# Five rearrangements around the mixer of a streaming trunk: the sample's recurrence in two units, half B's columns loaded in 320s, its decay later, cache copies and recurrences queued elsewhere

## The chip, the core and the metric

The kernel runs on one core of a Trainium2 chip. The metric is the device time of one execution in microseconds (us). The engines are TensorE (PE, with PEld its loads of weights), VectorE (DVE), ScalarE (ACT), GpSimd (POOL) and SyncE (SP), which here only issues transfers. Each engine works through its own instructions in a fixed order; a wait on one holds what stands behind it there.

## The reference

One step of a two-layer encoder on 1024 new prompt frames and 64 frames of a running stream (the sample). All is float32, model width 1024.

- Layer 0: one input projection feeds mixer A (RWKV-7: 8 heads of 64, a matrix state per head and a recurrence over the frames) and mixer B (GLA: gated linear attention over chunks of 64 frames). Their outputs, side by side, go through one output projection `w_out_mix`; then x <- LN(alpha x + f(x)), a SwiGLU with its own norm.
- Layer 1: banded softmax attention. The prompt's chunks see themselves and 8 chunks back; the sample sees a cache of 128 rows of K and V (`cache_c_k`, `cache_c_v`). Then projection, norm, SwiGLU, norm.

```python
p = x @ w_in_mix                                  # both mixers
ya, wkv, shift = rwkv7_time_mix(p[..., :A_PROJ], ...)
yb, gla        = gla_mix(p[..., A_PROJ:], ...)
x = layer_norm(ALPHA * x + concat([ya, yb]) @ w_out_mix)
x = layer_norm(ALPHA * x + swiglu(x, w_in, w_out))
```

## The kernel before

The frames are worked in two halves. Half A holds 384 prompt frames and the 64 sample frames (448 columns), half B the other 640 prompt frames (two banks of 320 columns). x is held transposed, in 8 tiles `kt` of 128 features, and every product with weights is exact to float32 by three matmuls on a high and a low part: xh wh, xl wh, xh wl (L124 to L126 with the weights stationary, L135, L136 and L138 with x stationary). ACT casts the high part (L101 for weights, L215 for x, L113 in a general `split`), DVE or POOL subtracts for the low part (L106 or L108, L216, L114).

`load_w` brings a weight tile (512 KB) into one of two raw buffers `wr`, and keeps four split ones. `load_xt(1)` uses the same two raw buffers for half B's x^T, 8 tiles of 640 columns (`xraw`, L214). Three of the 8 split tiles of half B have buffers of their own (`xeh`, `xel`); the other five take over the buffers of half A's x^T, so that their casts can be made only when half A's projection has read those.

The run of layer 0:

1. `inproj_rwkv(0)` and `inproj_gla(0)`: half A's projections. Beside them run the recurrences of half A as generators: `rwkv` takes units of work through the stages rw1 (decay, gates, L437 to L467), rw1b (products within a chunk, L484 to L497), rw2 (a triangular inverse by steps of pairs L549 and L551 on 16 partitions, fed by a round through DRAM: `l_d`, `lt`), rw3 (state and output, L607 to L642) and rw4 (transposition, L649, store to `yg_d`). A unit is a pair of heads `p` and two chunks of 64 frames. The sample has one chunk only: four units of one chunk each, whose inverse works on 8 partitions.
2. `inproj_gla(1)`, beginning with its decay branch (L352: a product with a low-rank matrix, its copy, then L363), then the q, k, v gemms; `inproj_rwkv(1)`.
3. `load_xt(0, yg_d)`: half A's mixer output comes back as x^T, `pack` copies the 64 sample columns, high and low, side by side into `xpk` (ACT L852, POOL L853), and `proj` multiplies with `w_om`, into the accumulators `acc` (L825 to L829). Four steps (`PRE`) of half B's recurrences are written ahead of it, the rest behind it.
4. `layer_norm` of half A, token tile by token tile (L884 to L897), with transposition (L902) and split (L113, L114) into x^T for the FFN of half A, during which half B's recurrences go on.
5. `cache_setup`, written in the FFN at j = 8: four loads of cached V into `cv` (one buffer, L1125), each split into `cvh` by ACT L113 and DVE L114 and stored (L1128); then K.

A scheduler takes the program as written and sets the order of each engine by its own model of times; a step may so land far from where it is written. `tc.issue_after(ins)` puts what a block traces behind the instruction `ins` on the engine of `ins`, without a wait. Before the change it isn't used at these places.

## Time and profile before

| | |
|---|---|
| runs | 3104.43, 3107.47, 3107.52 us; median 3107.47 |
| profiled execution | 3102.95 us; its span 3101.2 us |
| PE / PEld busy | 3007.5 / 2676.5 us |
| DVE / ACT / POOL busy | 2016.0 / 1270.8 / 1366.7 us |
| mean granted clock of TensorE | 0.977 of full speed |
| moved | 399 MB, 129 GB/s |

TensorE is busy nearly all the time; what a stage can still give is its waits and the stretches in which it runs at the lower clock. So the profile is read by stretches: where TensorE stood, what ended it, and at what clock it went on.

### The profile page before, as it was taken

What the parts mean: (1) busy time and instruction counts of PE and PEld (TensorE: products, weight loads), DVE (VectorE), ACT (ScalarE), POOL (GpSimd) and SP (SyncE); (2) the same over time, 40 slices, a digit from 0 to 9 for tenths busy, and PEclk for the clock granted to TensorE, in tenths of its full rate; (3) what the DMA queues carried; (4) which work ended last, traced back from release to release, by engine and by line L of the source; (5) the groups of instructions that cost most, each with busy time, mean ns of one, the idle gap of its engine ahead of it and who ended that gap; (6) DMA issues with size and microseconds to landing.
All of it is one profiled execution on the core that took longest, in us unless ns stands there. A gap on an engine that the chain in (4) does not pass through costs nothing.

```text
span 3101.2 us, 50069 instructions
## 1 busy us (share of the span) xinstructions
PE 3007.5 (97%) x17468; PEld 2676.5 (86%) x17468; DVE 2016.0 (65%) x4941; ACT 1270.8 (41%) x2761; POOL 1366.7 (44%) x1489
## 2 busy tenths in 40 slices
PE   8999999899999999999999999999999999899998
PEld 7888888688888888798999898898899988899987
DVE  5677875879898764455554466245566668866667
ACT  4454554344454334243443132355444434333322
POOL 2354534444454334343342233244445546654444
PEclk9999999889999999999999999999899999999999
DMA  6553334533533228343342222866454443322212
GB/s 195 148 161 115 109 110 124 146 104 106 151 105 106 91 97 294 118 153 120 113 134 98 82 95 101 247 200 175 121 153 135 117 175 122 122 86 80 98 68 75
DMA packets 298492, 399.29 MB, mean 129 GB/s; under 512 B 125504, under 2 KB 218552, under 8 KB 298240
## 3 DMA queue, kind: packets, MB, share of 16 engines
q1 hardware_dynamic: 297088, 393.48, 41.2%
q8 instruction: 138, 2.26, 0.3%
q10 hardware_dynamic: 1152, 2.62, 0.2%
q14 instruction: 114, 0.93, 0.1%
HBM read 323.63 MB, written 75.51 MB: 129 GB/s over the span
## 4 chain that ended last, share of the span: by engine, by line
PE 77%; DVE 8%; DMA 7%; POOL 2%; issue 2%; ACT 2%; SPq 1%; POOLq 0%; ACTq 0%; DVEq 0%
PE gps L124 11%; PE gps L126 11%; PE gps L125 11%; PE gps L135 7%; PE gps L136 7%; PE gps L138 7%; PE gps L1065 3%; PE gps L1066 3%; PE gps L1067 3%; PE op L1328 2%; PE tp L1302 2%; DVE t L549 1%; DVE x L551 1%; PE sps L1286 1%; PE sps L1287 1%
## 5 line engine op out<-in xcount | busy, mean ns | idle before, releaser
L108 POOL TENSOR_TENSOR wl<-wr,wh 128x512 fp32r<-128x512 f32 (+2 forms) x297 | 521.7, 1760 | 669.3 <-ACT wh L101 612.0
L124 PE MATMUL gps<-xh,wh 128*128 128x320 f32 (+1 forms) x2188 | 747.7, 342 | 12.5 <-ACT xh L215 6.0
L125 PE MATMUL gps<-xl,wh 128*128 128x320 f32 (+1 forms) x2188 | 746.5, 341 | 0.6 <-DVE xl L216 0.6
L126 PE MATMUL gps<-xh,wl 128*128 128x320 f32 (+1 forms) x2188 | 745.9, 341 | 0.3 <-DVE wl L106 0.2
L101 ACT CAST wh<-wr 128x1024 fp32r<-128x1024 f32 x360 | 375.6, 1048 | 465.9 <-PE gps L125 135.6
L106 DVE TENSOR_TENSOR wl<-wr,wh 128x512 fp32r<-128x512 f32 (+2 forms) x297 | 293.8, 990 | 242.2 <-ACT wh L101 239.8
L124 PEld LDWEIGHTS gps<-xh,wh 128*128 128x128 f32 x2188 | 415.6, 190 | 34.4 <-ACT xh L215 6.0
L126 PEld LDWEIGHTS gps<-xh,wl 128*128 128x128 f32 x2188 | 415.6, 190 | 18.6 <-issue 0.8
L125 PEld LDWEIGHTS gps<-xl,wh 128*128 128x128 f32 x2188 | 415.5, 190 | 18.3 <-DVE xl L216 1.0
L1297 POOL TENSOR_SCALAR s<-s,mx 128x640 f32<-128x640 f32 (+5 forms) x144 | 205.3, 1426 | 258.7 <-DVE mx L1296 236.3
L138 PE MATMUL gps<-wh,xl 128*128 128x512 f32 x661 | 258.9, 397 | 5.4 <-DVE xl L216 4.8
L135 PE MATMUL gps<-wh,xh 128*128 128x512 f32 x661 | 259.9, 399 | 3.9 <-DVE acc L829 1.9
L136 PE MATMUL gps<-wl,xh 128*128 128x512 f32 x661 | 261.5, 397 | 0.0
L135 PE MATMUL gps<-wh,hh 128*128 128x512 f32 x572 | 224.8, 396 | 1.6 <-ACT wh L101 1.3
L136 PE MATMUL gps<-wl,hh 128*128 128x512 f32 x572 | 225.5, 396 | 0.0
L827 DVE TENSOR_TENSOR acc<-acc,gps 128x512 f32<-128x512 f32 x216 | 143.6, 680 | 89.6 <-PE gps L138 82.3
L138 PE MATMUL gps<-wh,hl 128*128 128x512 f32 x484 | 189.6, 397 | 1.6 <-DVE hl L943 1.6
L549 DVE TENSOR_TENSOR t<-lt,x 16x48 f32<-16x48 f32 (+9 forms) x540 | 149.3, 276 | 36.0 <-DMA lt<-l_d 25.5
L1295 ACT ACTIVATE s<-s,mx 128x640 f32<-128x640 f32 (+5 forms) x144 | 96.4, 669 | 149.6 <-DVE mx L1294 145.2
L138 PEld LDWEIGHTS gps<-wh,xl 128*128 128x128 f32 x661 | 124.9, 189 | 33.8 <-DVE xl L216 5.4
L135 PEld LDWEIGHTS gps<-wh,xh 128*128 128x128 f32 x661 | 125.0, 190 | 32.8 <-issue 2.5
L136 PEld LDWEIGHTS gps<-wl,xh 128*128 128x128 f32 x661 | 125.2, 189 | 28.0 <-DVE wl L106 1.1
(406 smaller groups left out, 6312.0 us busy)
## 6 DMA issues: line engine op xcount, KB each, us to landing
wr<-in_w_fi SPq DMA_DIRECT2D x176, 512.0 KB
wr<-in_w_fo SPq DMA_DIRECT2D x88, 512.0 KB
wr<-in_w_in SPq DMA_DIRECT2D x44, 512.0 KB
wr<-in_w_qk SPq DMA_DIRECT2D x32, 512.0 KB
wr<-in_w_o SPq DMA_DIRECT2D x24, 512.0 KB
qs<-qd SPq DMA_DIRECT2D x32, 320.0 KB
wr<-in_w_om SPq DMA_DIRECT2D x16, 512.0 KB
wr<-in_w_v SPq DMA_DIRECT2D x16, 512.0 KB
```

Of the source, the lines that this page charges most:

```text
L101: self.A.copy(hi, raw)
L106: self.V.tensor_tensor(lo[:, :h], raw[:, :h], hi[:, :h].bitcast(F32), op=ALU.subtract)
L108: self.G.tensor_tensor(lo[:, h:], raw[:, h:], hi[:, h:].bitcast(F32), op=ALU.subtract)
L124: self.T.matmul(ps, hi[:, kt, :], xh, start=(kt == 0), stop=False)
L125: self.T.matmul(ps, hi[:, kt, :], xl, start=False, stop=False)
L126: self.T.matmul(ps, lo[:, kt, :], xh, start=False, stop=(kt == nk - 1))
L135: self.T.matmul(ps, xh, wh, start=(i == 0), stop=False)
L136: self.T.matmul(ps, xh, wl, start=False, stop=(lo is None and i == n - 1))
L138: self.T.matmul(ps, cols(lo(kt)), wh, start=False, stop=(i == n - 1))
L549: V.tensor_tensor(tv, lt[:, j, w:16].unsqueeze(2).to_broadcast([m, r, w]), x[:, 0, j, 0:w].unsqueeze(1).to_broadcast([m, r, w]), op=ALU.mult)
L827: self.V.tensor_tensor(a, a, ps[:m], op=ALU.add)
L1297: G.tensor_scalar(s[:m, :nk], s[:m, :nk], mx[:m, 3:4], None, op0=ALU.mult)
```

## The change

It has these parts:

- **Sample units.** The sample's four units become two, each of two pairs of heads; `rw1`, `rw3`, `rw4` and `rwkv` take a list of pairs (`u.segs`). The inverse of such a unit works on 16 partitions.
- **Half B's x^T** comes as 16 loads of 320 columns into 8 buffers of the pool `yr` instead of 8 loads of 640 into the two raw buffers of the weights.
- **Decay of half B** stands behind its four q and k gemms instead of ahead of them; half A's stays.
- **`pack`** copies in two halves of four `kt`, the later half first.
- **Recurrences of half B** behind the four first steps are queued on DVE behind `norms[-2]`, the last scaling (L897) of the third of four token tiles of the norm.
- **`cache_setup`** is queued on SP behind the last weight load that is written before it, and on ACT behind its cast.

```diff
@@ __init__
+        self.norms = []
@@ load_w
-        self.A.copy(hi, raw)
+        self.last_cast = self.A.copy(hi, raw).ins
@@ inproj_gla
+        def decay():
...
+        if hf == 0:
+            decay()
...
+        if hf:
+            decay()
@@ rw1
-    def rw1(self, sp, p, n, g0):
+    def rw1(self, sp, ps, n, g0):
...
-        u = SimpleNamespace(p=p, n=n)
-        pc = slice(128 * p, 128 * p + 128)
+        w = 64 * n
+        W = w * len(ps)
+        n *= len(ps)
+        u = SimpleNamespace(n=n, segs=[(p, slice(w * i, w * i + w)) for i, p in enumerate(ps)])
...
@@ rw3
-        G.tensor_copy(u.sv[0:64, 0], S)
+        step = n // len(u.segs)
+        for i, (p, _) in enumerate(u.segs):
+            G.tensor_copy(u.sv[0:64, i * step], S[p])
+        out = {}
...
@@ rwkv
-        units = [(p, n, 64 * c, 0) for c in range(0, (PA, NB)[hf] // 64, n) for p in range(4)]
+        units = [((p,), n, 64 * c, 0) for c in range(0, (PA, NB)[hf] // 64, n) for p in range(4)]
         if hf == 0:
-            units = [(p, 1, SMP, 1) for p in range(4)] + units
+            units = [((p, p + 1), 1, SMP, 1) for p in (0, 2)] + units
...
@@ pack
-        self.A.copy(xs[:, :, 0:64], xt.hi[:, :, SMP:])
-        self.G.tensor_copy(xs[:, :, 64:128], xt.lo[:, :, SMP:])
+        for ks in (slice(4, 8), slice(0, 4)):
+            self.A.copy(xs[:, ks, 0:64], xt.hi[:, ks, SMP:])
+            self.G.tensor_copy(xs[:, ks, 64:128], xt.lo[:, ks, SMP:])
@@ layer_norm
-                    V.scalar_tensor_tensor(a[:, c], a[:, c], rstd, gb[:m, 1, c], op0=ALU.mult, op1=ALU.add)
+                    self.norms.append(V.scalar_tensor_tensor(a[:, c], a[:, c], rstd, gb[:m, 1, c], op0=ALU.mult, op1=ALU.add).ins)
@@ run
-        self.load_xt(1)
+        for kt in range(8):
+            for c in (0, NB // 2):
+                self.load_xt(1, None, (kt,), slice(c, c + NB // 2), yp)
...
         self.proj(0, acc0, "w_om", self.layer_norm(0, acc0, "ln1", 0), pa)
-        for _ in r:
-            next(g, None)
-        for _ in g:
-            pass
+        with tc.issue_after(self.norms[-2]):
+            for _ in r:
+                next(g, None)
+            for _ in g:
+                pass
...
-                with tc.tile_pool(name="as", bufs=1) as asp:
+                with tc.tile_pool(name="as", bufs=1) as asp, tc.issue_after(self.last_w), tc.issue_after(self.last_cast):
```

(The cut parts of `rw1` to `rw4` repeat an operation for each entry of `segs` where it needs a pair's own constants.)

Where the scheduler now puts things: TensorE has 14899 rows for 14914, DVE 4843 instructions for 4943, and from 1123.7 us of the trace before (1120.5 for DVE) their rows are the same to the end. On SP, 14 of the 16 loads of half B's x^T stand behind the fifth and ahead of the tenth load of weights, where before they stood behind half A's last weights; the last two stand near the end of half A's projections. On TensorE between the two projections, before (L352 is the decay product of half B; the rest belongs to recurrences):

```order
L352 MATMUL gps<-xel,xaw 32x320 x2
L352 MATMUL gps<-xh_69,xaw 32x320 x2
L352 MATMUL gps<-xl_70,xaw 32x320 x2
L352 MATMUL gps<-xh_69,xaw 32x320 x2
L352 MATMUL gps<-xl_70,xaw 32x320 x2
L484 MATMUL pb<-ar,bbk 128x128 x2
L615 MATMUL ps<-rr,btt 64x64 x2
L352 MATMUL gps<-xh_69,xaw 32x320 x2
L582 MATMUL pz<-ys,t_1785 128x64
L584 MATMUL pz<-btt,yb 128x64
```

and after (L452 to L638 are the recurrences; L125 to L127 the gemms, L124 to L126 before):

```order
L127 MATMUL gps<-xh_69,wl 128x448
L452 MATMUL pa<-xg,w2z 128x128
L452 MATMUL pa<-xg,a2z 128x128
L452 MATMUL pa<-xg,g_209 128x128
L634 MATMUL ps<-uv,tok 64x64 x2
L637 MATMUL ps<-sv,ro 64x64
L638 MATMUL ps<-uv,arb 64x64
L637 MATMUL ps<-sv,ro 64x64
L638 MATMUL ps<-uv,arb 64x64
L590 MATMUL pz<-tt,lab 128x64 x2
L627 MATMUL ps<-sv,ro 64x64
L125 MATMUL gps<-xeh,wh 128x320
```

(the gemms L125 with xeh are half B's.) The decay product has gone from between the projections; half B's gemms follow half A's after some ten rows of recurrences.

On ACT at the copies of the cached V (`cvh`), just ahead of half A's output projection, before:

```order
L750 ACTIVATE gsq,gss<-gon 128x128
L113 CAST cvh<-cv 128x4x64
L613 COPY rr<-ps 64x128
L754 ACTIVATE gon<-gon,grstd 128x128
L113 CAST cvh<-cv 128x4x64
L441 ACTIVATE th<-pa,w0h 128x128
L443 ACTIVATE tha<-pa,a0h 128x128
L445 COPY gt<-pa 128x128
L215 CAST xh_69<-yraw 128x448
```

and after, where the scheduler has them in the FFN of half A (L102 is the cast of weights):

```order
L102 CAST wh<-wr 128x1024
L770 COPY gon<-gps 128x128
L738 ACTIVATE geb<-gb 128x64
L102 CAST wh<-wr 128x1024
L114 CAST cvh<-cv 128x4x64
L773 ACTIVATE gsq,gss<-gon 128x128
L579 COPY btt<-t_9350 64x2x64 x2
L632 ACTIVATE uv<-ps 64x128
L601 COPY btt<-btt 64x2x64
L777 ACTIVATE gon<-gon,grstd 128x128
L114 CAST cvh<-cv 128x4x64
```

The four casts have moved some 250 rows later, and L441 to L445, the gates of a recurrence, no longer stand behind one.

On DVE in the layer norm of half A, before (L549, L551: the inverse; L884 to L897: the norm; L827: the projection's accumulation):

```order
L549 TENSOR_TENSOR t_7243<-lt,x_7242 16x28
L886 BN_AGGR mv<-bs 128x2
L884 BN_STATS bs<-acc 128x6
L551 TENSOR_TENSOR x_7242<-x_7242,t_7243 16x2x14
L892 SCALAR_TENSOR_TENSOR acc<-acc,mv,gb 128x512 x2
L549 TENSOR_TENSOR t_7243<-lt,x_7242 16x15
L587 COPY_PREDICATED btt<-u_191,pz 128x2x64
L758 SCALAR_TENSOR_TENSOR gy<-gpy,gnwh,gsg 128x128
L897 SCALAR_TENSOR_TENSOR acc<-acc,rstd,gb 128x512
L827 TENSOR_TENSOR acc<-acc,gps 128x512
L551 TENSOR_TENSOR x_7242<-x_7242,t_7243 16x15
L520 TENSOR_TENSOR bon<-pt,rkv 128x128
```

and after (L908 to L921 are the norm, L850 the accumulation):

```order
L910 BN_AGGR mv<-bs 128x2
L916 SCALAR_TENSOR_TENSOR acc<-acc,mv,gb 128x512 x2
L850 TENSOR_TENSOR acc<-acc,gps 128x512
L921 SCALAR_TENSOR_TENSOR acc<-acc,rstd,gb 128x512
L416 TENSOR_TENSOR yb<-pz,bdk 128x256
L908 BN_STATS bs<-acc 128x6
L850 TENSOR_TENSOR acc<-acc,gps 128x512
L908 BN_STATS bs<-acc 128x6
L910 BN_AGGR mv<-bs 128x2
L916 SCALAR_TENSOR_TENSOR acc<-acc,mv,gb 128x512 x2
L600 COPY_PREDICATED btt<-u_191,pz 128x2x64
L645 SCALAR_TENSOR_TENSOR S<-sv,ec,ps 64x64 x2
```

The rows of the inverse have gone from between the rows of the norm, up to the third tile's L921; from there on they stand between them again. From the first accumulation L825 to the last L114 of the norm DVE has 138 rows instead of 169.

## Rows read from the trace of the kernel before

**Rows 1.** The page: the line of TensorE (busy time, share of the span, instructions), and the clock granted to it in 40 equal slices of the span, in tenths of full speed.

```profile
PE 3007.5 (97%) x17468; PEld 2676.5 (86%) x17468; DVE 2016.0 (65%) x4941; ACT 1270.8 (41%) x2761; POOL 1366.7 (44%) x1489
...
PEclk9999999889999999999999999999899999999999
```

**Rows 2.** Windows of the span, cut where TensorE changes its work. Columns: the stretch, its length, busy time (and instructions) of PE, PEld, DVE, ACT and POOL, the granted clock, the busy share of the DMA engines, GB/s.

```profile
32.00:100.00 68.00, 67.84 (x321) 58.64 (x321) 37.99 (x105) 32.63 (x55) 21.60 (x21) 0.97 0.57 161
168.75:194.43 25.68, 20.97 (x133) 15.06 (x132) 20.11 (x60) 15.18 (x46) 17.64 (x32) 0.91 0.54 172
194.43:201.00 6.57, 6.57 (x30) 6.57 (x30) 6.44 (x13) 5.93 (x11) 5.13 (x8) 0.58 0.38 124
...
532.40:537.90 5.50, 0.67 (x3) 0.25 (x2) 3.45 (x9) 3.95 (x11) 2.35 (x1) 1.00 0.16 34
537.90:548.30 10.40, 10.40 (x44) 8.18 (x44) 8.12 (x32) 1.68 (x7) 4.48 (x6) 0.84 0.77 92
548.30:564.50 16.20, 6.39 (x30) 5.39 (x29) 7.18 (x24) 5.11 (x17) 4.06 (x10) 0.60 0.74 192
564.50:606.30 41.80, 41.73 (x218) 34.35 (x219) 39.33 (x100) 14.99 (x40) 20.39 (x25) 0.99 0.52 151
606.30:641.00 34.70, 28.76 (x140) 22.80 (x139) 30.38 (x78) 16.09 (x47) 23.35 (x30) 0.55 0.33 115
641.00:900.00 259.00, 257.40 (x1610) 223.31 (x1609) 224.42 (x742) 121.40 (x364) 126.09 (x203) 0.99 0.41 119
```

**Rows 3.** What TensorE waited for in the first 1130 us: the waiting operation and line, what it waited for, us in total, times, the longest.

```profile
PE pb L484 <- ACT gt L445: 10.4, 2, 8.1
...
PE pz L582 <- ACT ys L580: 4.8, 3, 4.4
PE gps L138 <- DVE xl L216: 4.8, 1, 4.8
```

**Rows 4.** The same view of 168 to 195 us alone.

```profile
PE pb L484 <- ACT gt L445: 2.4, 1, 2.4
PE gps L352 <- DVE xl L216: 1.0, 1, 1.0
PE gps L352 <- POOL xl L216: 0.8, 1, 0.8
```

**Rows 5.** The timeline of TensorE (start, length, line, operation, output<-inputs): the last matmul of half A's input projection, and the first of half B's.

```profile
168.55 0.37 PE L126 MATMUL gps<-xh,wl 128*128 128x448 f32 x1
...
194.43 0.64 PE L124 MATMUL gps<-xeh,wh 128*128 128x320 f32 x1
```

**Rows 6.** The tile xraw, the raw columns of half B (count, shortest/median/longest ns, first and last start).

```profile
L214 SPq DMA_DIRECT2D xraw<-in_xt x8: 333/355/432, 151.6 to 175.8; - x8
...
L216 DVE TENSOR_TENSOR xl<-xraw,xh x2: 812/819/826, 169.6 to 176.7; 128x640 fp32r<-128x640 f32 x2
```

**Rows 7.** The timeline of ACT around 550 us, with the idle time before an instruction and what ended it.

```profile
555.61 0.40 ACT L113 CAST cvh<-cv 128x256 fp32r<-128x256 f32 x1 [11.90 <-DMA cv<-in_ck_v]
...
556.43 0.26 ACT L445 COPY gt<-pa 128x128 f32<-128x128 f32 x1
556.97 0.56 ACT L215 CAST xh<-yraw 128x448 fp32r<-128x448 f32 x1 [0.27 <-DMA yraw<-yg_d]
```

**Rows 8.** The timeline of the queue of SyncE there: the load on which the cast at 555.61 stands.

```profile
551.14 0.43 SPq L1125 DMA_DIRECT2D cv<-in_ck_v  x1
```

**Rows 9.** The timeline of VectorE there.

```profile
556.04 0.43 DVE L114 TENSOR_TENSOR cvh<-cv,cvh 128x256 fp32r<-128x256 f32 x1 [9.47 <-ACT cvh L113]
```

**Rows 10.** The timeline of TensorE at the end of the output projection of half A.

```profile
606.87 0.39 PE L439 MATMUL pa<-xg,g 128*128 128x128 f32 x2
611.65 1.12 PE L582 MATMUL pz<-ys,t 128*128 128x64 f32 x4 [4.39 <-ACT ys L580]
...
641.50 0.57 PE L124 MATMUL gps<-xh,wh 128*128 128x448 f32 x1
```

**Rows 11.** The timeline of VectorE there: the last accumulation of the projection and the last low part of the layer norm's x^T.

```profile
617.53 0.69 DVE L829 TENSOR_TENSOR acc<-acc,gps 64x512 f32<-64x512 f32 x1
...
641.16 0.39 DVE L114 TENSOR_TENSOR xl<-tps,xh 128x256 fp32r<-128x256 f32 x1
```

**Rows 12.** Groups of VectorE instructions of the first 1130 us, different shapes apart (partitions x elements, count | busy us, mean ns | idle before): one step of the triangular inverse, on 16 and on 8 partitions.

```profile
L549 DVE TENSOR_TENSOR t<-lt,x 16x63 f32<-16x63 f32 x64 | 16.5, 258 | 1.3
...
L549 DVE TENSOR_TENSOR t<-lt,x 8x63 f32<-8x63 f32 x8 | 3.8, 474 | 0.2
...
L549 DVE TENSOR_TENSOR t<-lt,x 8x39 f32<-8x39 f32 x8 | 1.5, 189 | 0.2
```

**Rows 13.** The queue of SyncE early in the span: two loads of weights.

```profile
30.45 1.41 SPq L98 DMA_DIRECT2D wr<-in_w_in  x2
```

**Rows 14.** ACT there: the cast of the first of them.

```profile
35.61 1.05 ACT L101 CAST wh<-wr 128x1024 fp32r<-128x1024 f32 x1 [1.92 <-DMA wr<-in_w_in]
```

**Rows 15.** POOL: the low parts of weights in this part of the span (count, shortest/median/longest ns, first and last start).

```profile
L108 POOL TENSOR_TENSOR wl<-wr,wh x9: 2357/2401/2412, 28.1 to 107.5; 128x1024 fp32r<-128x1024 f32 x9
```

**Rows 16.** TensorE: the first matmul with the first of them.

```profile
43.30 0.36 PE L124 MATMUL gps<-xh,wh 128*128 128x448 f32 x1
```

**Rows 17.** TensorE at its first use of the packed columns.

```profile
564.28 0.76 PE L135 MATMUL gps<-wh,xpk 128*128 128x512 f32 x1 [0.16 <-POOL bk L468]
```

More of the change, by code (lines that the diff above doesn't have):

```diff
@@ L341, in inproj_gla @@
         n, c0, xt = self.N[hf], self.base[hf], self.xt[hf]
-        raw = pool.tile([128, 8, 16], F32, tag="xar", name="xar", bufs=1)
-        nc.sync.dma_start(raw, self.a["w_xa"])
-        whl = pool.tile([128, 8, 32], F32R, tag="xaw", name="xaw", bufs=1)
-        A.copy(whl[:, :, 0:16], raw)
-        V.tensor_tensor(whl[:, :, 16:32], raw, whl[:, :, 0:16].bitcast(F32), op=ALU.subtract)
-        segs = self.banks(hf)
-        for kt in range(8):
-            for i, xx in enumerate((xt.h(kt), xt.l(kt))):
-                for ps, s0, w in segs:
-                    T.matmul(ps[0:32, :], whl[:, kt, :], xx[:, s0 : s0 + w], start=(kt + i == 0), stop=(kt + i == 8))
@@ L444, in rw1 @@
-        u.gt = st("gt", bufs=5)
+        th, tha, kkn = st("th", bufs=2), st("tha"), st("kkn")
+        u.gt = st("gt", bufs=5)
+        for p, cs in u.segs:
+            pc = slice(128 * p, 128 * p + 128)
+            for i, (m, x) in enumerate(((self.w2z, 0), (self.a2z, 0), (self.g2, 1))):
+                T.matmul(pa[:, W * i + cs.start : W * i + cs.stop], m[:, pc], xg[:, x, :], start=True, stop=True)
+        for p, cs in u.segs:
+            A.activation(th[:, cs], pa[:, cs], AF.Tanh, bias=self.w0h[:, p : p + 1], scale=0.5)
+            A.activation(tha[:, cs], pa[:, W + cs.start : W + cs.stop], AF.Tanh, bias=self.a0h[:, p : p + 1], scale=0.5)
@@ L472, in rw1b @@
     def rw1b(self, sp, u):
-        V, A, G, T, p, n = self.V, self.A, self.G, self.T, u.p, u.n
+        V, A, G, T, n = self.V, self.A, self.G, self.T, u.n
         W = 64 * n
@@ L622, in rw3 @@
                 T.matmul(o, u.arb[:, c, h, :], u.uv[0:64, c, h, :], start=False, stop=True)
-            S2 = u.sv[0:64, c + 1] if c + 1 < n else sp.tile([64, 2, 64], F32, tag=f"S{p}", name="S", bufs=2)
+            p = u.segs[c // step][0]
+            if (c + 1) % step:
+                S2 = u.sv[0:64, c + 1]
+            else:
+                S2 = out[p] = sp.tile([64, 2, 64], F32, tag=f"S{p}", name="S", bufs=2)
             for h in range(2):
@@ L665, in one @@
         def one(i):
[L666 to L667 removed]
+            ps, m, c0, smp = units[i]
+            st[i] = self.rw1(sp, ps, m, self.base[hf] + c0)
         def three(i):
[L670 to L676 removed]
+            ps, m, c0, smp = units[i]
+            for p, s in self.rw3(sp, st[i], S).items():
+                S[p] = s
+                if smp:
+                    self.wkv_out(sp, s, self.a["s_wkv"][2 * p : 2 * p + 2])
+                    S[p] = self.state(sp, p, src)
+                elif hf == 0 and c0 == PA - 64 * n:
+                    self.nc.sync.dma_start(self.wkv_d[p].rearrange("(h k) v -> k h v", h=2), s)
         for i in range(len(units) + 4):
@@ L1373, in run @@
         self.xt[1] = self.xt_tiles_in(es_one.enter_context(tc.tile_pool(name="xb", bufs=1, side="right")), 8 - NA * 8 // NB)
-        self.load_xt(1)
+        for kt in range(8):
+            for c in (0, NB // 2):
+                self.load_xt(1, None, (kt,), slice(c, c + NB // 2), yp)
         self.inproj_gla(1, one)
```

95 lines of the change are left out of this document (46 added, 49 removed).

## The prediction

> **What bounds the kernel now.** I read the page first: TensorE is busy in 97% of the span, and its clock is down in only a few of 40 slices [rows 1]. So the time is TensorE's stream of matmuls plus what interrupts it. The change takes almost no matmul away; it is worth what it does to the interruptions. The page's averages can't show these, so I cut the span where TensorE changes its work [rows 2]. In each stretch two losses can be read: idle time (length less PE busy), and busy time B at a mean granted clock c, of which about B x (1 - c) is lost. Then the list of waits says what ended the idle time [rows 3].
>
> On TensorE the two orders are the same from 1123.7 us on, so everything must come from ahead of that. Four places stand out:
>
> - 168.75 to 201 us, between the two halves' projections: 4.7 us idle; 20.97 x 0.09 + 6.57 x 0.42 = 4.6 lost to the clock. Together 9.3.
> - 532.4 to 548.3 us: 4.8 idle behind a late low part of x^T [rows 3]; 10.40 x 0.16 = 1.7 to the clock. Together 6.5.
> - 548.3 to 564.5 us, ahead of half A's output projection: 9.8 idle; 6.39 x 0.40 = 2.6 to the clock. Together 12.4.
> - 606.3 to 641 us, half A's layer norm: 5.9 idle; 28.76 x 0.45 = 12.9 to the clock. Together 18.8.
>
> That is 47 us, and no more than this can well be won. After each of these idle times the clock is low and the next matmuls are longer, so when an idle time goes, part of the clock's loss goes with it.
>
> **The change, part by part.**
>
> *Decay and x^T of half B.* Half A's last gemm ends at 168.9, half B's first begins at 194.43 [rows 5]. Between them stand the decay product, recurrences, and waits of 2.4, 1.0 and 0.8 us, for a gate and for low parts of x^T [rows 4]. Those are late because xraw comes through two buffers, the last of its loads issued only at 175.8 [rows 6]. With the change 14 of 16 loads are in long before, and the gemms stand directly behind half A's. The decay's matmuls are still to be done; only the interruptions go. What is late next: five of the eight tiles can still be cast only when half A's last gemms have read the old ones. Two pieces of 320 columns cost DVE about what one of 640 does, 0.82 us [rows 6], shared with POOL, against some 0.8 us for the six matmuls that a tile feeds (30 of them took 6.57 us at a clock of 0.58 [rows 2], 0.13 each at full speed); they run nearly in step, and I leave 1.3 us of waits. Of 9.3 I take **-8**; the ends are -3 (the casts take the place of the waits) and -10.
>
> *The cached V.* ACT stands 11.90 us ahead of the cvh cast at 555.61 and DVE 9.47 behind it [rows 7, 9]; its load was issued only at 551.14 [rows 8], since cv has one buffer. Behind that cast stands L445, the gate that TensorE awaits for 8.1 us [rows 3, 7]. In the new order the cast has gone from there, and the loads of `acc` and of the norm's weights come earlier too. What is late next is the last tile of half A's mixer output, cast at 556.97 [rows 7]; its load stood behind the same queue. Of 12.4 I take **-11**; the ends are -5 (that tile stays late) and -13. The wait at 532.4 us, for a low part that stands behind a step of the inverse on DVE, has the same neighbours in the new order: -1, ends -5 and 0.
>
> *Recurrences behind the norm.* TensorE is through with the projection at 606.87 and reaches steady FFN gemms at 641.50 [rows 10]. DVE adds up the last piece only at 617.53 and delivers the last low part of x^T at 641.16 [rows 11]. So of the 34.7 us some 10.7 are DVE's lag behind TensorE, and 24 the end of the norm with recurrence steps in between. The change takes 31 DVE rows out, all ahead of the third tile's scaling; at 0.258 us each (a middle step of the inverse [rows 12]) that is 8 us. The end of the norm keeps its steps. So lag goes and end stays: **-8**. The ends are -2 (the lag is bound by TensorE in other places) and -14 (the wait of 4.39 at 611.65 [rows 10] and small matmuls at the low clock go as well). The 8 us of steps are made up in the FFN, where DVE has 259 - 224 = 35 us free [rows 2]: +2, ends 0 and +8 (all on the path).
>
> *Sample units.* 30 L549 and 30 L551 fall away. On 8 partitions a step took 0.19 to 0.47 us and on 16 it takes 0.26 [rows 12], no more for twice the heads. So DVE is relieved of 60 x 0.19 = 11 to 60 x 0.47 = 28 us. That lies at 90 to 200 us, where TensorE seldom waits for DVE (from 32 to 100 us it is busy in 67.84 of 68.00 us [rows 2]): **-1**, ends -4 and 0. On the relief, though not on the term, the Trainium skill says less: "VectorE: DVE Perf Modes", section on the TRN2 errata, gives 58 cycles at 0.96 GHz as what an operation costs beyond its elements, from which I estimate 60 x 0.06 = 4 us. The rows give at least 11.
>
> *Early loads.* Three of the x^T loads go ahead of the weights issued at 30.45 [rows 13]. Their cast begins at 35.61 and ends at 36.66, POOL's low part takes 2.4 us more, and TensorE uses them from 43.30 [rows 14 to 16]: about 4.2 us to spare. Three loads of 164 KB cost three issues of 0.36 us [rows 6] and, at the 161 GB/s at a DMA share of 0.57 [rows 2], so 282 at full, 1.7 us of transfer: 2.8 us, inside the margin. All 16, 2.6 MB, are 9.3 us of transfer, and 0.43 x 68 = 29 us are free. I take **+1**, ends 0 and +5. A rule of the Trainium skill speaks against this part: "DMA: Bandwidth & Descriptors", Rules for kernel authors, wants transfers large, and from its measured table (138 GB/s at 64 KB, 341 at 1 MB) I estimate 13 us for the 16, at some 200 GB/s. By that too the loads lie inside the 29, and the term stays.
>
> *The cached V, where it lands.* In the FFN each cast again stands behind a load through one buffer, 4.5 us from issue to cast [rows 7, 8]. ACT has 259 - 121 = 138 us free there [rows 2], and weights are split ahead: **+2**, ends 0 and +18 (four times 4.5).
>
> *`pack` in halves.* The first matmul with xpk waited 0.16 us, and for something else [rows 17]. What hides the copies is TensorE's own work ahead of that use; without this cover a change of half a copy could show. I take 0.
>
> Sum: -8 - 11 - 1 - 8 + 2 - 1 + 1 + 2 = **-24 us**. The profiled execution took 3102.95, 4.5 below the median of 3107.47; against the median I forecast **3083 us**.
>
> **The rivals.**
>
> 1. *The low clock goes too.* At the norm 12.9 us are lost to the clock. If TensorE has its gemms again soon enough to stay at the upper level, the good ends come: -10, -13, -5 (the wait at 532 with its clock) and -14, with the other terms' +4: -38, 3069. For it: the clock follows the idle times. Against it: the norm's end still offers TensorE only small matmuls.
> 2. *Gaps refill.* The half-A tile through DRAM is late by itself, the casts of half B take the place of the loads, and DVE is bound by the recurrences all the same: -3, -5, 0, -2, +2, 0, +1, +2 = -5, so 3102. For it: DVE is busy in 39.33 of 41.80 us ahead of the norm [rows 2]. Against it: the cv load is the named end of the largest wait.
> 3. *The cached V holds DVE in the FFN: slower.* DVE's cast stood 9.47 us [rows 9]. There DVE is busy in 224 of 259 us [rows 2] with steps on which TensorE's recurrences and the FFN's accumulation depend. Four holds of 9.5 are 38 us for 35 free, and all could come through: -24 - 2 + 38 = +12, 3119. It turns the sign from 26 / 4 = 6.5 us a hold on the path. Against it: a hold of 9.5 came from an issue that was late itself; a load then takes 4.5.
> 4. *The order as written by the scheduler doesn't hold the deferral:* the tail behind the third tile keeps its steps, so the norm gives nothing and the FFN takes nothing: -24 + 8 - 2 = -18, 3089. For it: the end of the norm does keep them. Against it: 31 rows are gone ahead of it.
>
> **How the numbers follow.** 0.2%, 6.2 us, is about what a measurement of this kernel can tell from no change. Forecast 0.57, rival 1 0.15, rival 2 0.15, rival 3 0.08, rival 4 0.05. Rival 2 straddles the bound at 3101.3: a third of it counts as faster. Faster: 0.57 + 0.15 + 0.05 + 0.05 = 0.82; same: 0.10; slower: 0.08, rival 3. The range reaches from a little below rival 1 to a little past rival 2, 3062 to 3106, which leaves out rival 3 and the ends beyond, some 0.15 to 0.2.
>
> **What would show it.** In the profile of the changed kernel: half B's first 320-column gemm within 5 us of half A's last; no wait of 8 us ahead of half A's projection, and no cv among ACT's waits there; the last low part of the norm some 27 us after the projection instead of 34; ACT's four waits for cv in the FFN below 5 us, with no TensorE wait behind them; from the end of that FFN on, everything earlier by the same amount. I am wrong if the FFN of half A becomes longer by more than 5 us, or if the 320-column gemms wait for their casts by more than 5.

## The result, and the profile after

The change makes the kernel slower: 3113.49 us (median of 20 runs, 3104.97 to 3123.25) against 3107.49 (20 runs), a ratio of 1.0019 [1.0012, 1.0026]. That is +6.0 us where -24 was forecast, and outside the range. The profiled execution after took 3118.2, 4.7 above its median, where that of before lay 4.5 below its own. So the two traces differ by 15.3 us, 9 more than the medians, and only large differences between them mean something.

The page after, the lines that answer to [rows 1]. The slices below 9 are now the second, the sixth and the ninth (from 78, 390 and 623 us on), where before they were the eighth and ninth; the 29th is below 9 in both.

```profile
PE 3008.8 (97%) x17460; PEld 2671.4 (86%) x17460; DVE 1995.0 (64%) x4841; ACT 1268.3 (41%) x2742; POOL 1358.7 (44%) x1470
...
PEclk9899989989999999999999999999899999999999
```

Windows, with the columns of [rows 2], cut in both kernels where TensorE has issued the same number of large matmuls; so the rows of the two fences are pairs. First before, then after.

```profile
97.50:108.50 11.00, 11.00 (x60) 10.22 (x59) 3.23 (x8) 9.21 (x13) 5.14 (x6) 1.00 0.65 104
...
163.90:208.70 44.80, 40.09 (x239) 33.56 (x238) 34.39 (x93) 30.57 (x73) 28.48 (x42) 0.89 0.53 165
...
231.50:268.60 37.10, 37.02 (x223) 30.67 (x222) 26.31 (x104) 14.41 (x49) 14.27 (x32) 1.00 0.33 100
...
332.60:402.90 70.30, 68.24 (x511) 59.62 (x510) 61.72 (x237) 37.06 (x124) 36.76 (x71) 1.00 0.40 112
...
532.00:582.80 50.80, 36.16 (x171) 29.75 (x171) 34.92 (x104) 19.19 (x57) 22.13 (x32) 0.83 0.70 168
582.80:646.40 63.60, 57.59 (x284) 46.46 (x283) 56.37 (x150) 23.87 (x65) 34.54 (x46) 0.73 0.31 95
646.40:940.00 293.60, 292.00 (x1840) 251.17 (x1839) 258.24 (x844) 136.34 (x412) 144.33 (x231) 0.99 0.41 118
```

```profile
100.20:122.10 21.90, 14.48 (x64) 12.81 (x63) 8.31 (x19) 12.36 (x23) 6.55 (x10) 0.77 0.39 84
...
182.80:208.80 26.00, 26.00 (x182) 23.42 (x180) 18.53 (x57) 14.75 (x41) 14.23 (x23) 1.00 0.52 153
...
231.00:274.50 43.50, 42.66 (x252) 33.63 (x252) 32.67 (x122) 27.06 (x73) 21.35 (x41) 0.84 0.28 78
...
352.00:438.70 86.70, 83.16 (x554) 70.78 (x553) 64.51 (x259) 40.34 (x133) 37.02 (x75) 0.88 0.32 91
...
556.50:606.00 49.50, 36.71 (x170) 28.29 (x171) 27.79 (x76) 14.72 (x39) 15.67 (x19) 0.86 0.65 128
606.00:663.40 57.40, 46.53 (x250) 36.92 (x249) 52.66 (x124) 21.84 (x58) 35.38 (x46) 0.82 0.32 94
663.40:948.00 284.60, 284.01 (x1780) 244.58 (x1779) 250.08 (x818) 134.00 (x403) 138.04 (x219) 1.00 0.46 126
```

Read with the prediction's two losses, idle time plus B x (1 - c), the pairs give, before to after: 0 to 10.7; 9.1 to 0; 0.1 to 7.7; 2.1 to 13.5; 20.8 to 17.9; 21.6 to 19.2; 4.5 to 0.6. The differences are +10.7, -9.1, +7.6, +11.4, -2.9, -2.4 and -3.9, in sum +11.4 of the 15.3. So the gap between the projections went, and three stretches pay for it: a new wait at 110 us, and a low clock where the decay's small matmuls (231 us) and the recurrences (352 us) now stand.

TensorE's longest waits in the first 1130 us after (columns of [rows 3]):

```profile
PE pb L497 <- DVE bbk L416: 11.5, 2, 7.4
PE gps L136 <- issue: 8.3, 1, 8.3
```

The first, in the timelines of DVE and of TensorE after: DVE stood 12.74 us for a load of rkv, and TensorE behind it 7.42.

```profile
108.81 0.28 DVE L458 SCALAR_TENSOR_TENSOR kkn<-rkv,vec,rsb 128x64 f32<-128x64 f32 x1 [12.74 <-DMA rkv<-rkv_d]
```

```profile
110.83 1.41 PE L497 MATMUL pb<-ar,bbk 128*128 128x128 f32 x5 [7.42 <-DVE bbk L416]
```

That load had been issued at 94.94. The queue of SyncE after, and the DMAs issued from 90 to 112 us (count, KB each, us from issue to landing):

```profile
93.12 0.43 SPq L1403 DMA_DIRECT2D out_dram<-shS  x1
93.64 0.84 SPq L99 DMA_DIRECT2D wr<-in_w_gv  x1
94.94 0.37 SPq L436 DMA_DIRECT2D rkv<-rkv_d  x1
```

```profile
wr<-in_w_gv SPq DMA_DIRECT2D x1, 512.0 KB, 14.8
...
rkv<-rkv_d SPq DMA_DIRECT2D x1, 96.0 KB, 13.8
...
out_dram<-shS SPq DMA_DIRECT2D x1, 7.0 KB, 13.6
```

The store ahead of them writes `shS`, the shift column, 128x14 values that lie singly in the output: 1792 pieces of 4 bytes. It takes 13.6 us for 7 KB, and all behind it lands 13 to 15 us after its issue.

The second wait is at the start of half A's output projection. TensorE after, and the DMAs issued from 560 to 585 us:

```profile
583.41 0.76 PE L136 MATMUL gps<-wh,xpk 128*128 128x512 f32 x1 [8.34 <-issue]
```

```profile
wr<-in_w_om SPq DMA_DIRECT2D x1, 512.0 KB, 15.6
```

At 563.93 the twin store, `shP`, is issued, and the projection's weights and all else again stand behind it. Before has it too, in the very place where I had put a wait of 8.1 us down to the load of cv. The queue of SyncE before:

```profile
540.44 0.42 SPq L1378 DMA_DIRECT2D out_dram<-shP  x1
540.97 1.83 SPq L98 DMA_DIRECT2D wr<-in_w_om  x1
549.68 0.36 SPq L427 DMA_DIRECT2D rkv<-rkv_d  x1
```

From 542.8 to 549.68 the queue issues nothing. The cv load at 551.14 [rows 8] was late because of that. What the queue itself waits for, from 540 to 560 us, the view of its waits says (columns of [rows 3]):

```profile
SPq L427 <- DMA rkv_d<-xs: 6.8, 1, 6.8
```

That is a store of 320 KB to `rkv_d`, issued at 539.88, half a microsecond ahead of the scattered one, and the load at 549.68 reads back what it wrote. So the scattered store here slowed also what was issued just ahead of it and was still on its way; with the stores of the first experiment below this wait is 1.3 us. At 92.75 us in the kernel after it did not: a store of 224 KB issued 0.37 us ahead of `shS` landed in 2.1 us.

### The profile page after: what moved, and what is told of

The parts are those of the page before. It is cut to its first block, busy times and chain, and to the rows that moved or that the text cites. A ratio compares the mean times of both kernels' runs of the same rounds, so it can differ in the third digit from the quotient of the medians.

```text
span 3116.5 us, 49917 instructions
## 1 busy us (share of the span) xinstructions
PE 3008.8 (97%) x17460; PEld 2671.4 (86%) x17460; DVE 1995.0 (64%) x4841; ACT 1268.3 (41%) x2742; POOL 1358.7 (44%) x1470
## 4 chain that ended last, share of the span: by engine, by line
PE 75%; DMA 9%; DVE 8%; issue 2%; POOL 2%; ACT 2%; SPq 1%; POOLq 0%; DVEq 0%; ACTq 0%
PE gps L125 10%; PE gps L127 10%; PE gps L126 10%; PE gps L136 8%; PE gps L137 8%; PE gps L139 7%; PE gps L1089 3%; PE gps L1090 3%; PE gps L1091 3%; PE op L1352 2%; PE tp L1326 2%; DMA wr<-in_w_in 2%; DVE t L562 1%; DVE x L564 1%; PE sps L1310 1%
## 5 line engine op out<-in xcount | busy, mean ns | idle before, releaser
L125 PE MATMUL gps<-xh,wh 128*128 128x320 f32 (+1 forms) x2188 | 745.1, 341 | 12.4 <-ACT xh L216 5.9
L127 PE MATMUL gps<-xh,wl 128*128 128x320 f32 (+1 forms) x2188 | 744.3, 340 | 0.2 <-POOL wl L109 0.2
L126 PE MATMUL gps<-xl,wh 128*128 128x320 f32 (+1 forms) x2188 | 743.9, 340 | 0.6 <-DVE xl L217 0.6
L102 ACT CAST wh<-wr 128x1024 fp32r<-128x1024 f32 x360 | 375.8, 1048 | 473.9 <-PE gps L126 135.8
L125 PEld LDWEIGHTS gps<-xh,wh 128*128 128x128 f32 x2188 | 413.9, 189 | 35.8 <-ACT xh L216 5.9
L127 PEld LDWEIGHTS gps<-xh,wl 128*128 128x128 f32 x2188 | 413.7, 189 | 18.8 <-POOL wl L109 0.8
L126 PEld LDWEIGHTS gps<-xl,wh 128*128 128x128 f32 x2188 | 413.5, 189 | 18.4 <-DVE xl L217 1.0
L1321 POOL TENSOR_SCALAR s<-s,mx 128x640 f32<-128x640 f32 (+5 forms) x144 | 205.4, 1426 | 256.2 <-DVE mx L1320 233.2
L850 DVE TENSOR_TENSOR acc<-acc,gps 128x512 f32<-128x512 f32 x216 | 143.3, 679 | 91.0 <-PE gps L139 84.7
L562 DVE TENSOR_TENSOR t<-lt,x 16x15 f32<-16x15 f32 (+7 forms) x510 | 129.8, 255 | 34.6 <-DMA lt<-l_d 24.7
```

The source lines that it names most:

```text
L102: self.last_cast = self.A.copy(hi, raw).ins
L125: self.T.matmul(ps, hi[:, kt, :], xh, start=(kt == 0), stop=False)
L126: self.T.matmul(ps, hi[:, kt, :], xl, start=False, stop=False)
L127: self.T.matmul(ps, lo[:, kt, :], xh, start=False, stop=(kt == nk - 1))
L562: V.tensor_tensor(tv, lt[:, j, w:16].unsqueeze(2).to_broadcast([m, r, w]), x[:, 0, j, 0:w].unsqueeze(1).to_broadcast([m, r, w]), op=ALU.mult)
L850: self.V.tensor_tensor(a, a, ps[:m], op=ALU.add)
```

## The experiments

Times are medians of 4 to 11 runs, and ratios, with their 95% intervals, are to the kernel before, run beside them on the same chip (there its median was 3103.25, 3103.59, 3103.43, 3104.55 or 3104.92 us). A ratio isn't the quotient of the two medians and lies up to 0.12% from it, so differences between kernels are taken from the ratios. My theory from these traces: the scattered stores hold everything behind them. The rival: the change's own new order does the harm, and the stores lie beside it.

**The stores as 128 runs of 14 numbers** ("flat" from here on), in the kernel after and in that before. The numbers then stand at other places of the output, so these kernels only serve to measure.

```diff
-        nc.sync.dma_start(a["s_shift"].rearrange("c p -> p c"), self.shS)
+        nc.sync.dma_start(a["s_shift"].rearrange("c p -> (c p)").rearrange("(p c) -> p c", c=14), self.shS)
... the same for p_shift
```

> The changed kernel with the two stores of the shift columns (128 partitions x 14 numbers each, written as 1792 single numbers 512 bytes apart) written as 128 runs of 14 numbers instead (the same bytes, at permuted places). Theory 1 (what stands on SP's queue behind such a store lands only when the store is through, 13.6 us; the change moved a sample load and the output projection's weights right behind the two stores): the 12.7 us hold of DVE before the sample's L458 and the 8.3 us wait of TensorE before the first packed product go, 15 to 25 us less than the changed kernel, about 3090 to 3100. Theory 2 (the loss is in the recurrences' own order, above all 360 to 440 us): within 4 us of the changed kernel, 3110 to 3117.

> The kernel before with the same two stores as 128 runs each; every engine's order stays as it was. Theory 1: the wait of 8.1 us ahead of half A's output projection, which I had put down to the load of the cached V, was a wait behind the second store; it shrinks to below 3 us, and the time falls by 6 to 14 us, to 3093 to 3101. Theory 2 and my prediction's reading (the one buffer of cv): the wait stays at 6 us or more, and the time is within 3 us of 3107.

After: 3102.89 us, 0.9999 [0.9987, 1.0011], some 3 us above what I had expected; the store lands in 2.0 us, and the wait at 110 us and that for the projection's weights are gone. Before: 3097.07, 0.9983 [0.9967, 0.9999], and there the order on TensorE and on SyncE's queue is the same to the last row. TensorE in that kernel, where before waited 8.08 us at 556.75:

```profile
549.92 1.34 PE L484 MATMUL pb<-ar,bbk 128*128 128x128 f32 x8 [2.17 <-ACT gt L445]
```

The queue of SyncE there goes on after 1.3 us:

```profile
539.28 0.42 SPq L1378 DMA_DIRECT2D out_dram<-shP  x1
539.80 1.84 SPq L98 DMA_DIRECT2D wr<-in_w_om  x1
542.95 0.37 SPq L427 DMA_DIRECT2D rkv<-rkv_d  x1
```

So the wait that I put down to cv's buffer was the store's: nothing of cv was changed here. It costs the kernel before 0.17%, 5 us. For the change the step is 0.20%, but this isn't the store's price alone: from the start of half A's output projection on (583 us) the traces show another order on TensorE than in the change, some 2800 of 17460 rows at other places. Against the kernel before with the same stores the change still stands 0.16% higher, 5 us, but the two intervals reach 0.12% and 0.16% to either side, so this remainder isn't clear of noise.

**The sample's two units alone**, with the usual and then with flat stores.

```diff
+            units = [((p, p + 1), 1, SMP, 1) for p in (0, 2)] + units
... with rw1 to rw4 as in the change; x^T, decay, norm, cache, pack as before
```

> The kernel before with the sample's recurrence in two units, and nothing else of the change. In its order the load of the second sample unit stands right behind the first store of shift columns. Theory 1: DVE is held some 12 us near 108 us as in the changed kernel, TensorE 7 us and then a stretch at the low clock; 3112 to 3122. My prediction's reading: -1 us, so 3103 to 3108.

> The kernel before with the sample's recurrence in two units alone, and the two stores of shift columns as 128 runs of 14 numbers (at permuted places). With the old stores the sample's two units cost 17 us (3120). Theory 1 alone: what is left is nothing, within 3 us of the kernel before with these stores, 3094 to 3100. Theory 1 with theory 2 (half the loss is the hold behind the first store, half the recurrences at 365 to 445 us, which stand there with fewer gemms beside them): 3103 to 3109, with 8 to 12 us more excess than before at 365 to 445 us.

3119.95 us, 1.0049 [1.0034, 1.0064]: the worst of all kernels by its ratio, by one part that I had at -1. With flat stores, the order on TensorE and on SyncE's queue alike: 3101.78, 0.9990 [0.9980, 0.9999]. The wait, in the timeline of TensorE with the usual stores:

```profile
108.09 2.04 PE L494 MATMUL pb<-ar,bbk 128*128 128x128 f32 x8 [7.64 <-DVE bbk L413]
```

The load behind it, in the DMAs of 90 to 112 us, with the usual and with flat stores:

```profile
rkv<-rkv_d SPq DMA_DIRECT2D x1, 96.0 KB, 11.5
```

```profile
rkv<-rkv_d SPq DMA_DIRECT2D x1, 96.0 KB, 3.2
```

The store's part in this loss is shown: it costs this kernel 0.59% by the ratios, 18 us, where it costs the kernel before 0.17%. With two units for four, the second unit's load of rkv stands close behind the store, with one load of weights between them, and is awaited at once. So of the 0.49%, 15 us, that the two units cost with the usual stores, 0.07%, 2 us, is left when both kernels have flat ones, and that is within the intervals. But in the trace the later recurrences lose more with the two units, whatever the stores. Windows of the kernel before with flat stores, and of this one, the pair of 332.60:402.90 above:

```profile
332.70:402.90 70.20, 68.21 (x511) 59.59 (x510) 61.82 (x238) 37.05 (x124) 36.72 (x71) 1.00 0.41 114
```

```profile
352.90:437.80 84.90, 80.11 (x536) 66.39 (x535) 64.55 (x250) 39.14 (x126) 32.53 (x67) 0.90 0.33 90
```

2.0 us lost against 4.8 + 8.0.

**All but the sample's units**: the change with one unit for each pair of heads.

```diff
-            units = [((p, p + 1), 1, SMP, 1) for p in (0, 2)] + units
+            units = [((p,), 1, SMP, 1) for p in range(4)] + units
```

> The changed kernel with the sample's recurrence in four units as before, all other edits kept. Its order has no rkv load right behind the first store. Theory 1: no hold of DVE near 108 us; against the changed kernel 8 to 16 us less, 3098 to 3106, with the wait behind the second store kept at 6 us or more. Theory 2 (later recurrences): the loss at 360 to 440 us stays, 3106 to 3114.

3100.61 us, 0.9990 [0.9979, 1.0001]. The cv loads are in the FFN here, and yet TensorE waits ahead of half A's projection, for longer than before:

```profile
563.55 0.66 PE L522 MATMUL pt<-ident,bk 128*128 128x128 f32 x2 [12.22 <-DVE arb L510]
```

Moving cv removed nothing of this wait. Against the change, 1.0019, this kernel is 0.29% lower, 9 us: taking the sample's two units out takes the whole loss away.

**x^T and decay; x^T alone.** The parts of the diff in `load_xt`'s loop and `inproj_gla`.

```diff
+        if hf:
+            decay()
...
+                self.load_xt(1, None, (kt,), slice(c, c + NB // 2), yp)
```

> The kernel before with two edits: half B's x^T in 320 columns, and its decay behind the q and k gemms. Theory D (moving the decay only moves the interruption: recurrences stand without gemms beside them where the decay now is): 10 us won between the projections, 6 to 10 lost at 230 to 270 us, so within 4 us of the kernel before, 3100 to 3107. My prediction: -7, 3096.

> The kernel before with half B's x^T in 320 columns alone; the decay stays ahead of half B's gemms. Theory D: the waits for the low parts go (some 2 to 3 us), the clock's loss between the projections stays, and nothing is lost at 230 to 270 us: 3099 to 3103. If instead the late x^T made the interruption: most of the 9 to 10 us are won without the decay's move, 3092 to 3096.

Both: 3103.81, 1.0006 [0.9997, 1.0015]. x^T alone: 3109.43, 1.0016 [1.0007, 1.0026]. Windows of both parts together, to be read beside 163.90:208.70 and the decay's new place:

```profile
165.90:187.60 21.70, 20.72 (x133) 18.62 (x132) 15.19 (x32) 12.29 (x34) 13.62 (x18) 1.00 0.50 160
214.70:247.20 32.50, 31.10 (x162) 24.07 (x162) 24.23 (x87) 21.23 (x53) 16.45 (x32) 0.84 0.33 93
```

Before lost 9.1 us in the first stretch, this kernel 1.0. In the second it loses 1.4 + 5.0 where before lost about nothing. There TensorE does the matmuls of the decay and of the recurrences, part of them at the lower clock. So the gap was moved more than removed: -8 as forecast, and some 6 given back where those matmuls went. Without the decay's move the early columns cost 0.16%, 5 us, which neither side of my expectation had. The gap stays, TensorE is busy in 49.09 of the 51 us from 163 to 214 at a clock of 0.83, and the later recurrences lose some 4 us more (windows at the end of the next section).

**The cached V in the FFN, and the recurrences queued behind the norm, each alone on the kernel before with flat stores.**

```diff
+                with tc.tile_pool(name="as", bufs=1) as asp, tc.issue_after(self.last_w), tc.issue_after(self.last_cast):
... or, in the other kernel
+        with tc.issue_after(self.norms[-2]):
```

> The kernel before with the cached V queued in the FFN, and the two stores of shift columns as 128 runs of 14 numbers (at permuted places). Beside the same stores without the move of the cached V (3097.1). My prediction's reading (cv's one buffer made the wait of TensorE ahead of half A's output projection): the 2.2 and 1.7 us that are left of it go, and some clock: -4 to -8, 3089 to 3093. Theory 1 (the store made it, the cv load was one of those that it held): -2 to +4, 3095 to 3101.

> The kernel before with half B's later recurrences queued on DVE behind the third scaling of the norm, alone, and the two stores as 128 runs of 14 numbers (at permuted places). Beside the same stores without it (3097.1). My prediction: -8 at the norm, +2 in the FFN, so -6, 3091. Theory N (the end of the norm is bound by small matmuls at the low clock, and the recurrences only move into the FFN): -4 to 0 at the norm, given back in the FFN; within 3 us of 3097.

Cached V: 3101.66, 0.9991 [0.9980, 1.0002]. Norm queue: 3099.09, 0.9978 [0.9969, 0.9988]. Against the 0.9983 [0.9967, 0.9999] that flat stores give alone, neither can be told from nothing. Windows of the projection's end and the norm, cut at the same large matmuls, without the norm queue and with it:

```profile
589.20:638.90 49.70, 43.77 (x213) 34.92 (x212) 42.99 (x111) 21.38 (x57) 29.05 (x39) 0.66 0.32 93
588.40:639.90 51.50, 41.55 (x213) 33.40 (x213) 44.23 (x116) 22.24 (x62) 30.80 (x42) 0.67 0.29 86
```

The rows of the inverse have gone from between those of the norm, and yet the stretch is no shorter: idle time and clock cost 20.8 us there without the queue and 23.7 with it.

**The shift columns turned by TensorE and stored as 14 rows of 512 bytes**, in three kernels.

```diff
+            nc.tensor.transpose(ps[0:14, 0:128], col, self.ident)
+            nc.scalar.copy(row, ps[0:14, 0:128])
+            nc.sync.dma_start(a[name], row)
```

> The change without the sample's two units, and the shift columns turned by TensorE (128x14 to 14x128, one small matmul and one copy each) and stored as 14 rows of 512 bytes. Theory 1 (a store of single numbers holds what is issued behind it): the wait of 12.2 us ahead of half A's output projection goes to below 4; against the same kernel with the old stores (3100.6) some 8 to 14 us less, 3086 to 3093. Rival (that wait is one of the chain of half A's last recurrences): no more than 3 us less, 3097 to 3101.

> The kernel before with the shift columns turned by TensorE and stored as 14 rows of 512 bytes; all outputs in place. Theory 1: the wait ahead of half A's output projection shrinks as with 128 runs; 3092 to 3101, if the scheduler's order stays about as good. Against it: the new matmul and copy change the order around the norm, as in the run without the sample's units, which cost 14 us there; then 3103 to 3115.

> As the run before, with the cached V queued in the FFN as well. Theory 1: 3090 to 3100; against the run before -4 to +2.

All but the sample: 3112.46, 1.0030 [1.0014, 1.0046]. Before: 3109.71, 1.0019 [1.0010, 1.0029]. Before with the cached V moved: 3108.81, 1.0021 [1.0010, 1.0032]. All three came out above what theory 1 had. The wait ahead of half A's projection is below 3 us in all of them, but the few added instructions let the scheduler write another order for the norm behind it, and that costs more: in the first, 40 us of the norm (600 to 640) have TensorE busy in 23.46 at a clock of 0.56. So these three say nothing on the store's price. They show that a few instructions added ahead of the norm can move this kernel by as much as the change did.

**The stores issued from ACT's queue.**

```diff
-        nc.sync.dma_start(a["s_shift"].rearrange("c p -> p c"), self.shS)
+        nc.scalar.dma_start(a["s_shift"].rearrange("c p -> p c"), self.shS)
... the same for p_shift
```

> The kernel before, with the two stores of shift columns (1792 single numbers each, as before) issued from ACT's queue instead of SP's; TensorE's order is unchanged. If the hold is one of SP's own ring: as with 128 runs, the wait ahead of half A's output projection falls from 8.1 and 1.6 us to about 2.2 and 1.7, and the time to 3094 to 3100. If the DMA engines themselves are taken, whatever the ring: the wait stays above 6 us, 3101 to 3106.

> The changed kernel with the two stores issued from ACT's queue. Own ring: no hold of DVE near 108 us; 3098 to 3105, as with 128 runs (3102.9). Engines taken: the hold at 108 us stays above 8 us, and the time within 4 us of the changed kernel, 3105 to 3114.

> The change without the sample's two units (3100.6 with the old stores), the stores issued from ACT's queue. Own ring: the wait of 12.2 us ahead of half A's output projection falls below 5, 3088 to 3095, unless the order at the norm turns out worse, as it did with the 14 rows. Engines taken: 3098 to 3103.

Before: 3101.96, 0.9995 [0.9984, 1.0005], with the wait still at 8.3 us. After: 3120.62, 1.0041 [1.0028, 1.0054]. All but the sample: 3102.78, 0.9993 [0.9980, 1.0006]. The first and third came as the side of the engines had it; in the second DVE's hold came so too, with 9.80 us, but the time is 6 us above the range of both sides and 0.22% above the change itself. The DMAs of the second, 92 to 114 us:

```profile
q10 hardware_dynamic: 1808, 0.01, 4.6%
...
rkv<-rkv_d SPq DMA_DIRECT2D x1, 96.0 KB, 10.2
...
out_dram<-shS ACTq DMA_DIRECT2D x1, 7.0 KB, 12.6
```

The store's packets have a queue to themselves now, and the load on the other still takes 10.2 us (3.7 in the change with flat stores). So it isn't the place in the queue that costs, but the time in which the store runs. The Trainium skill says why one might expect that, in "DMA: Bandwidth & Descriptors", section "Issuing engines are not separate DMA queues": transfers from all issuing engines end on the same 16 DMA engines. The trace agrees, with these 10.2 us.

The second kernel has TensorE's order of the change with flat stores (all but 78 of 17460 rows at the same place) and stands 0.42% above it, 13 us. That is the store's price in this order, with the sample's two units in it.

**The scattered writing later**: flat to a scratch at the old place, and from there, single numbers again, in half B's first FFN.

```diff
-        nc.sync.dma_start(a["s_shift"].rearrange("c p -> p c"), self.shS)
+        nc.sync.dma_start(self.sh_d[0], self.shS)
...
+            if j in (1, 4):
+                with tc.issue_after(self.last_w):
+                    nc.sync.dma_start(a["ps"[j == 1] + "_shift"].rearrange("c p -> p c"), self.sh_d[j != 1])
```

> The kernel before; the shift columns go to a scratch in DRAM as 128 runs of 14 numbers, and are put into the output's order from there, single numbers again, while half B's layer 0 is in its FFN. The outputs are the reference's. If the scattered store harms only by what stands behind it: the wait of 8 us before half A's projection is down to about 2, no new wait of more than 3 us comes up where the late copies run, and the time is that of the kernel before with flat stores, 3094 to 3100 us. Rival: the late copies hold weights there for about 12 us each, and TensorE waits for them: 3102 to 3112 us.

> The whole change but the sample's units, with the same late reordering of the shift columns. If the store hid what moving cv is worth and nothing else was amiss: the wait before half A's projection is gone and the time is 8 to 12 us under that of the same kernel with the usual stores, 3088 to 3095 us, faster than the kernel before by 0.2 to 0.5%. Rival: something else is late next there (the column norms, as with x and the cached V alone), and the time stays at 3097 to 3103 us.

> The whole change, with the same late reordering. If the store alone turned the change into a loss: no wait of 7 us at 110 us, the time that the change with flat stores took, 3098 to 3106 us, or the kernel before's within 0.2%. Rival: the loss of the sample's two units is theirs and the flat stores only hid it: 3110 us or more.

Before: 3101.30, 1.0000 [0.9988, 1.0011]. All but the sample: 3101.20, 0.9991 [0.9982, 1.0001]. The whole change: 3107.28, 1.0008 [0.9995, 1.0022]. My expectation failed for the first two. For the second the rival's range came; the first lies between the two ranges, but what the rival had said of TensorE came too. The third lies 1 us above my range, within 0.2% of the kernel before. The early wait is gone, but the copies were issued at 1341 and 1426 us, and behind the first of them TensorE waits 5.51 us at 1362; behind the second it waits for nothing up to 1450. Windows of the kernel before with flat stores, and of the first of these:

```profile
1340.00:1440.00 100.00, 99.33 (x620) 91.65 (x618) 52.35 (x153) 40.67 (x99) 39.12 (x41) 1.00 0.44 136
```

```profile
1340.00:1440.00 100.00, 94.49 (x588) 88.17 (x587) 49.01 (x142) 39.19 (x94) 33.30 (x36) 0.97 0.48 121
```

So the scattered store is moved, not hidden. The three, run beside each other, give an account without the early store, by the ratios: all but the sample against before -0.09%, the sample on top +0.17%, 5 us, together +0.08%, which isn't clear of noise. So the sample's two units cost 0.07 to 0.17% without the early scattered store, and 0.29 to 0.49% with it: the loss is for the most part that of the two together. What is left of the change without that store, 0.08 to 0.16%, isn't clear of noise. No version of these is shown to beat the kernel before with outputs in their places; the one with all but the sample is nearest, at -0.1% with an interval that touches none.

## Why the prediction was wrong

- **The cached V, -11**: the step that failed first. I had read the name at the end of a wait (the cast on cv) as its cause, without following the queue back. The load was late because the queue behind the store of `shP` issued nothing for 7 us. Flat stores took the wait from 8.08 to 2.17 us with cv where it was; with cv moved and the stores as they were it was 12.22. Moved alone beside equal stores, cv gave 0.9991 against 0.9983 and 1.0021 against 1.0019. The term is about 0 where -11 stood, and what the store costs there stays in the changed kernel, as 8.34 us for the weights.
- **The sample's units, -1, ends -4 and 0**: wrong in sign. I counted DVE's steps and not what the order puts behind what on SyncE's queue. With two units the second one's rkv load comes to a place close behind the store of `shS`. They cost 0.49%, 15 us, alone and 0.29%, 9 us, within the change. With the store out of the way 2 us (flat) to 5 us (later) are left by the ratios, and the clock that is low between 350 and 440 us.
- **Decay and x^T, -8**: the gap closed as forecast (9.1 to 0 us; the first gemm of 320 columns starts 2.6 us behind the end of half A's last, with no wait), but I let the decay's matmuls cost nothing where they go. With the recurrences they make a stretch in which part of the time is at the lower clock: +7.6 in the trace after, some +6 with these two parts alone. The later recurrences lose some 5 us more as well. The net of these two parts is +0.06% [-0.03, +0.15], where -7 us, -0.23%, stood with the early loads.
- **The norm, -8 + 2**: -2.4 and -3.9 in the traces, nothing measurable alone. From the projection's last matmul to the last low part it took 35 us before and 31 after, where 27 was forecast; with the norm queue alone it took 37, against 35 without. So the 31 rows don't set DVE's lag by themselves.
- **The stall at 532 us, -1**: 4.8 us before, 1.7 and 1.4 after, at 558.86 and 563.08: about right.
- **Early loads +1**: the early columns alone cost 5 us, the upper end of this term, but not where I had priced it: up to 60 us TensorE waits 1.1 us in all for casts of weights there, 3.0 before.
- **cv in the FFN +2, pack 0**: not refuted. ACT's waits for cv in the FFN come to 5.3 us in three, the longest 3.63, and no TensorE wait hangs on them that I could find; in the FFN's stretch TensorE loses 0.6 us where before lost 4.5, so rival 3 didn't happen.

What was measured of the sum: all parts but the sample's units gave -0.10% [-0.21, +0.01], -3 us, where -23 stood; the units on top gave +9 us, where -1 stood; together +6. How the -3 us divide among the other parts isn't shown. Rival 2, that gaps refill, was nearest in kind. Its price had no term for a store that holds the queue, nor for a low clock in a new place.

**What stays open**: why TensorE runs at the lower clock for part of the recurrences from 350 to 440 us, with the sample's units alone as with the whole change. The stretch holds 25 to 43 instructions more than before, but no run changed that alone. Two parts of the change make this stretch dearer, each alone. Windows of the kernel before, of x^T alone and of the sample's two units alone, all with the usual stores:

```profile
330.00:480.00 150.00, 145.88 (x1062) 129.46 (x1062) 124.00 (x470) 77.79 (x236) 65.06 (x122) 0.98 0.41 114
330.00:480.00 150.00, 142.76 (x1023) 125.76 (x1022) 120.63 (x464) 75.81 (x230) 66.42 (x119) 0.97 0.40 112
330.00:480.00 150.00, 141.84 (x1013) 122.37 (x1012) 113.42 (x423) 74.43 (x227) 60.02 (x119) 0.95 0.37 102
```

Idle time and clock cost 7.0, 11.5 and 15.3 us there. Over all 20 traces, one of each kernel, it is 4.1 to 8.4 us in the eight with neither part, 8.0 to 12.3 in the six with early x^T, alone or with other parts but the sample's two units, and 14.8 to 18.8 in the six with the two units. Open too is what of these 10 us each execution has: the medians say less than the traces.

## What to carry to other kernels

When a wait ends with a load, follow that load's queue back, to what the queue itself waited for and to the transfers that ran then: how long they take decides, and their size in bytes doesn't tell it. When small matmuls are moved out of a gap, price the place where they go at the clock that similar stretches have, not at nothing. An edit that takes work off an engine also moves every later load on the issuing queue, and this must be read in the order before a term is written down.

## What the runs showed of the hardware

A store of 1792 single numbers of 4 bytes took 11.8 to 13.6 us; the same 7 KB as 128 runs of 56 bytes took 1.9 to 3.6. While the first ran, loads of 96 to 512 KB landed 10 to 16 us after their issue, on the same queue and on another alike (rkv, 96 KB: 11.5 us, and 3.2 beside a flat store in the same order). The Trainium skill, "DMA: Bandwidth & Descriptors", Rules for kernel authors, has a strided last dimension lowered to a descriptor for each element. The trace agrees: 1808 packets for the store's queue, where it had one to itself.

TensorE's clock went to its lower level, 1.2 GHz, in a stretch where it had hardly stood: 42.66 of 43.50 us busy, and 0.84 granted. In the timeline of TensorE after, the same two matmuls take 0.32 us there and, a little behind waits of 0.27 and 0.57, 0.47:

```profile
247.22 0.32 PE L638 MATMUL ps<-uv,arb 64*64 64x64 f32 x2
...
250.38 0.45 PE L627 MATMUL ps<-sv,ro 128*64 128x64 f32 x4 [0.27 <-DVE sv L645]
...
251.40 0.44 PE L631 MATMUL ps<-rr,btt 64*64 64x64 f32 x4 [0.57 <-ACT rr L629]
...
253.84 0.47 PE L638 MATMUL ps<-uv,arb 64*64 64x64 f32 x2
```

The row of the 13 us from 252.6 on shows the level, half of full speed with TensorE busy throughout:

```profile
252.60:265.90 13.30, 13.30 (x45) 9.40 (x46) 6.83 (x28) 9.28 (x21) 5.00 (x13) 0.50 0.26 65
```

The prediction had the clock follow the idle times, and priced none where there was no gap. What brought it down here no run isolates.
